# Attention on one core: VectorE's exponential in four instructions, ten groups instead of nine, and two banks for the last head

## The chip, the cores and the metric

The kernel runs on one core of a Trainium2 chip. A core has engines that run their own instruction streams in order and meet at semaphores: TensorE (PE; PEld is its weight load), VectorE (DVE), ScalarE (ACT), GpSimd (POOL) and SyncE (SP, which here only issues DMAs). SBUF is the working memory, PSUM holds what TensorE writes, in banks of 2 KB per partition. The metric is device time in microseconds (us); lower is better.

## The reference

Plain softmax attention over 8 x 8 heads, 512 queries and keys, 64 dimensions, all float32:

```python
scale = 1.0 / np.sqrt(q.shape[-1])
scores = np.einsum('bhqd,bhkd->bhqk', q, k) * scale
scores = scores - scores.max(axis=-1, keepdims=True)
attn = np.exp(scores)
attn = attn / attn.sum(axis=-1, keepdims=True)
return np.einsum('bhqk,bhkd->bhqd', attn, v)
```

The inputs are standard normal draws, and the kernel leaves out the subtraction of the maximum: it takes the exponential of the scaled score as it is, and divides at the end.

## The kernel before

**Tiles.** Heads go in 32 pairs `g` of two heads `h`. Per pair q, k and v are loaded by SP (256 KB each, up to seven pairs ahead), cast to float16 on GpSimd (`cast`, L435 and L445), and q and k are transposed on TensorE (L469); VectorE copies the transposed pair from PSUM to the tile `tqk` (L482). The scores of one head are taken with keys on the partitions, so one key block `c` of 128 keys gives a 128 x 512 block of scores, one bank. Two such blocks make a group `m`, a PSUM tile `st` of two banks (128 x 1024), and there are three such tiles. There are 128 groups; the last is done as two halves of 256 queries, so `m` runs to 128.

**The exponential** of a group is one ACTIVATE on ScalarE (L516) that writes the float16 tile `pt`. The groups listed in `ON_DVE` go to VectorE instead. For them TensorE first adds a constant to the scores by two matmuls of a constant tile `lift` (L497), and VectorE then runs `raise_` (L536), a multiply and a maximum that turns `st` into a float tile `z` whose upper bits are the exponent and whose lower 16 bits are a fraction f. That instruction releases the score tile. After it come the passes (L553), each a `scalar_tensor_tensor` over 128 x 1024 elements. Before the change there are four: y = (f + c0) f, y = (y + c1) f, y = (y + c2) f, and y c3 + z, whose result, stored as an unsigned integer in the tile `pd`, has in a 16-bit half of each word the float16 exponential.

**Values.** The float16 blocks are the weights of matmuls against v with a column of ones beside it (L588), so 65 columns come out: 64 dimensions and the sum. A unit is 128 queries of one head, four matmuls; seven units fill a bank, and VectorE's `normalise` then takes the reciprocal of the sums (L566) and multiplies (L568) into `ring`. For each finished head SP stores 128 KB. The last head is treated apart: `last_values` (L603) writes its four units as parts 0 to 3 into a score tile, parts 0 and 1 for key blocks 0 and 1 of all queries, part 2 for blocks 2 and 3 of the first 256 queries, part 3 for those of the last 256. `finish` (L617, L618) normalises each half, and its store goes out on SP's queue for the first half and on ScalarE's for the second.

**What sets the order.** The class `Plan` simulates the engines with fixed costs in nanoseconds, and the steps that it notes are emitted in that order for all engines. Its constants steer it:

- `PASS`, `PASSES` are the planned cost and number of passes of a group on VectorE.
- `KEEN` keeps the values of any head back until group number `m` has passed it.
- `CALM`: a cast planned after that time is given a wait on VectorE's latest instruction; one planned earlier starts when its data is there.
- `LATE_NORM`, `LATE_COPY`: VectorE begins a pass only if no norm or raise (copy) that is known to come would then be made later than this. In `step_dve`, `end` is the planned end of the pass, and all `ready` entries `x` must have `x[0] > end - late[x[1]]`.
- `BACKLOG`: TensorE waits up to `SOON` (80) for a score tile if ScalarE's planned work in hand is less than this.
- A pair with a group in `ON_DVE` has its v cast due 6000 later (`late` in `__init__`), and SP's later loads follow the casts.

In `last_values` before the change all four units share one bank of the score tile `o_last`.

Of the kernel before, what the change touches and what calls it, by code (L numbers as in the profile page):

```python
# [17 lines left out]
class Plan:  # L18
# [6 lines left out]
    COPY, NORM, RAISE = (601, 690), (307, 390), (1132, 1215)  # L25
    COPY_1 = (400, 190)
    NORM_COLUMN, PASS_DONE = 67, 80
    PASS, PASSES = 1133, 4
    OFFSET = 216
    FIRST_EXP = 4915  # L30
    STEP = 5
    CALM, KEEN = 9000, 4
    FIRST_UNIT = 4
    ON_DVE = (8, 24, 35, 41, 61, 68, 80, 94, 111)

    LATE_NORM, LATE_COPY, HURRY, SOON, BACKLOG = 1300, 1400, 900, 80, 1000
    SLACK, AHEAD = 0, 1

    CAST, CAST_DONE, TO_POOL = 557, 130, 150
# [3 lines left out]
    def __init__(self, groups, pairs, first):  # L43
# [26 lines left out]

        late = {grp[0][0] for m, grp in enumerate(groups) if m in self.ON_DVE}
        due = []
# [75 lines left out]
    def for_dve(self, m):  # L148
        return m in self.ON_DVE

# [192 lines left out]
def kernel(  # L343
# [7 lines left out]
    nc = tc.nc  # L351
    B, H, S, D = q.shape
    P = 128
    NI = S // P
    assert NI == 4 and D == 64 and S == 512
    scale = float(D) ** -0.5
# [45 lines left out]
    last = {}  # L402

    def source(src, g):
        b, h = g // ppb, 2 * (g % ppb)
        return src[b, h : h + 2].rearrange("h (p i) d -> p h i d", i=NI)
# [45 lines left out]
    def dve(ins):  # L452
        latest[:] = [ins]
        return ins
# [32 lines left out]
    def scores(m, on_dve):  # L487
# [35 lines left out]

    LIFT, STEP = (793.0 / 32, -0.039614853593207044 / 32), scale * 1.4426950408889634 * 1024
    QUARTIC = tuple(
        x * 65536.0**n
        for n, x in enumerate((-22.8615461, 17.9701791, 3.89093568)[::-1], 1)
    ) + (1.34267018e-02 * 1024 * 2.0**-64,)  # L530

    def raise_(m):
        r = raised[m]
# [12 lines left out]
    def pass_(m, s):  # L546
        r = raised[m]
        f = r["z"].bitcast(U16).rearrange("p x (s n) -> p x s n", n=2)[:, :, :, 0]
        if s == 0:
            r["y"] = wpool.tile([P, 2, S], FP32, tag="y", name=f"y_{m}")  # L550
        last = s == 3
        dve(
            nc.vector.scalar_tensor_tensor(  # L553
                out=r["bits"][:, :, :] if last else r["y"][:, :, :],
                in0=r["y"][:, :, :] if s else f,
                scalar=QUARTIC[s],
                in1=r["z"][:, :, :] if last else f,
                op0=AluOp.mult if last else AluOp.add,
                op1=AluOp.add if last else AluOp.mult,
            )  # L560
        )
# [34 lines left out]
    def last_values(part):  # L596
        if part == 0:
            o = ps_st.tile([P, 2, S], FP32, tag="st", name="o_last")
            last["o"] = o[:, 0, 0 : NI * (D + 1)].rearrange("p (x d) -> p x d", x=NI)
        o = last["o"]  # L600
        for c in (part,) if part < 2 else (2, 3):
            for x in (range(NI), range(NI), (0, 1), (2, 3))[part]:
                nc.tensor.matmul(  # L603
                    o[:, x, :],
                    blocks[(LAST, c, 1)][:, x * P : (x + 1) * P],
                    vps[LAST % NV][:, 1, c, :],
                    start=(c == 0 and x == 0),
                    stop=(c == NI - 1),
                    skip_group_check=True,
                )  # L610

    def finish(part):
        o = last["o"]
        n = slice(2 * part - 4, 2 * part - 2)
        ob = opool.tile([P, 2, D], FP32, tag="obl", name=f"obl_{part}")
        rc = opool.tile([P, 7, 1], FP32, tag="rc", name=f"rc_last_{part}")
        nc.vector.reciprocal(out=rc[:, 0:2], in_=o[:, n, D : D + 1])  # L617
        nc.vector.tensor_tensor(  # L618
            out=ob[:, :, :],
            in0=o[:, n, 0:D],  # L620
            in1=rc[:, 0:2].broadcast_to([P, 2, D]),
            op=AluOp.mult,
        )
        queue = (nc.sync, nc.scalar)[part - 2]
        queue.dma_start(out=source(out, LAST)[:, 1, n], in_=ob[:, :, :])
# [101 lines left out]
    with tc.manual_schedule():  # L727
        plan = Plan(groups, NP, 3)
        steps = plan.run()
        first_loads()  # L730
        for g, name in plan.first_loads:
            load(g, name)
        make_identity(nc, ident)
        nc.vector.memset(lift, LIFT[0])
        for p in (32, 96):
            nc.vector.memset(lift[p : p + 32], LIFT[1])
        for n in range(NV):
            nc.vector.memset(vps[n][:, :, :, D : D + 1], 1.0)
        first_pair()
        do = {  # L740
            "transposes": transposes,
            "scores": scores,
            "values": values,
            "load": load,
            "cast": cast_behind,
            "raise": raise_,
            "copy": lambda g, b: copy(g),
            "pass": pass_,
            "last": last_values,
            "finish": finish,  # L750
            "norm": lambda u, n, b: normalise(u, n),
        }
        for what, *args in steps:
            do[what](*args)
# [30 lines left out]
```

## Time and profile before

| what | value |
|---|---|
| time, three runs | 120.11, 120.23, 120.72 us; median 120.23 |
| profiled execution: its own time, as its span from first to last instruction | 118.6 us |
| TensorE busy | 105.0 us (89%) |
| VectorE busy | 103.7 us (87%) |
| ScalarE busy | 111.6 us (94%) |
| GpSimd busy | 57.5 us (48%) |
| HBM traffic | 25.17 MB read, 8.39 MB written, 283 GB/s |
| mean granted TensorE clock | 0.993 |

The profile is of one execution, and the page gives no other time for it than the span. Its groups name line, engine, operation, tile written <- tiles read, shape and count; behind the bar stand busy time, the mean duration of one instruction in ns, and the idle time of the engine just before them with what ended it. In the timeline the first two numbers are start and duration in us from the start of the span, xN says how many instructions are merged, and brackets give idle time before. Instructions of one engine overlap at their ends, so a duration is a little longer than the step from one to the next.

### The profile page before, as it was taken

Reading aid. Unit: us, or ns where it says so; the run is one execution under the profiler, and the core shown is the slowest. Engines: PE = TensorE matmul, PEld = TensorE weight load, DVE = VectorE, ACT = ScalarE, POOL = GpSimd, SP = SyncE. Lnnn points to the kernel's source line nnn. Section 1 sums busy time; section 2 is a strip of 40 time slices with the busy share of each in tenths; the row PEclk is TensorE's granted clock in tenths of the full one; section 3 lists DMA queues with packets and bytes.
Section 4 is the critical chain, followed back from the end, with each engine's and each line's share of the span. In section 5 each row is a group of like instructions: output and inputs, shape, how many; then the busy total and the mean of one; then the engine's idle time right before and its main releaser. Section 6 shows DMA issues by size and latency. Waiting matters only on the chain.

```text
span 118.6 us, 4088 instructions
## 1 busy us (share of the span) xinstructions
PE 105.0 (89%) x1577; PEld 66.4 (56%) x1577; DVE 103.7 (87%) x179; ACT 111.6 (94%) x124; POOL 57.5 (48%) x102
## 2 busy tenths in 40 slices
PE   7969987999799897989989998998899998998960
PEld 2626554755466454658545574675465674755750
DVE  3453999799999999998999999999999999998560
ACT  4699999999999999999999999999999999999960
POOL 2378731991547722555947255533645436524000
PEclk9999999999999999999999999999999999999997
DMA  3999999999999999999889957999899874231344
GB/s 101 305 352 380 378 380 383 383 379 378 367 302 326 350 365 355 327 371 358 250 297 275 299 169 255 342 364 293 266 309 373 275 253 164 91 122 63 109 163 134
DMA packets 35607, 33.83 MB, mean 285 GB/s; under 512 B 2691, under 2 KB 35587, under 8 KB 35587
## 3 DMA queue, kind: packets, MB, share of 16 engines
q1 hardware_dynamic: 35152, 33.24, 84.8%
q10 hardware_dynamic: 432, 0.33, 0.8%
q8 instruction: 12, 0.20, 0.8%
q14 instruction: 11, 0.07, 0.2%
HBM read 25.17 MB, written 8.39 MB: 283 GB/s over the span
## 4 chain that ended last, share of the span: by engine, by line
ACT 34%; PE 28%; DVE 16%; DMA 11%; issue 6%; SPq 1%; POOL 1%; ACTq 0%
ACT pt L516 32%; PE o L588 10%; PE st L511 10%; DMA k<-in_k_dram 8%; DVE y L553 5%; PE tp L469 4%; DVE tqk L482 3%; DVE ring L568 3%; DMA out_dram<-ring 3%; PE st_0a L636 3%; ACT pt L686 2%; DVE z L536 1%; DVE rc L566 1%; DVE pd L553 1%; SPq L429 1%
## 5 line engine op out<-in xcount | busy, mean ns | idle before, releaser
L516 ACT ACTIVATE pt<-st 128x1024 f16<-128x1024 f32 (+1 forms) x117 | 106.7, 1200 | 0.1
L511 PE MATMUL st<-tqk 64*128 64x512 f16 (+1 forms) x250 | 45.3, 379 | 7.1 <-ACT pt L516 5.4
L588 PE MATMUL o<-vp,pt 128*128 128x65 f16 x936 | 41.7, 194 | 0.0
L588 PEld LDWEIGHTS <-pt 128*128 128x128 f16 x936 | 35.4, 98 | 11.2 <-issue 8.5
L445 POOL CAST qkp<-k 128x512 f16<-128x512 f32 x31 | 19.1, 616 | 20.1 <-DVE y L553 5.5
L435 POOL CAST vp<-v 128x512 f16<-128x512 f32 x32 | 19.7, 619 | 16.6 <-DVE y L553 9.7
L511 PEld LDWEIGHTS <-tqk 64*128 64x128 f16 x250 | 13.7, 93 | 20.9 <-issue 13.8
L445 POOL CAST qkp<-q 128x512 f16<-128x512 f32 x30 | 18.5, 616 | 12.0 <-DVE y L553 7.0
L568 DVE TENSOR_TENSOR ring<-o,rc 128x448 f32<-128x448 f32 (+2 forms) x37 | 22.6, 612 | 1.3
L553 DVE SCALAR_TENSOR_TENSOR y<-y,z 128x1024 f32<-128x1024 f32 x18 | 22.1, 1228 | 0.0
L469 PE MATMUL tp<-ident,qkp 128*128 128x128 f16 x248 | 20.1, 220 | 0.9 <-DVE tqk L482 0.4
L482 DVE COPY tqk<-tp 128x1024 f16<-128x1024 f16 x30 | 20.5, 682 | 0.3 <-PE tp L469 0.3
L469 PEld LDWEIGHTS <-qkp 128*128 128x128 f16 x248 | 14.4, 97 | 8.9 <-issue 4.3
L553 DVE SCALAR_TENSOR_TENSOR y<-z 128x1024 f32<-128x1024 uint16 x9 | 12.1, 1340 | 0.0
L536 DVE TENSOR_SCALAR z<-st 128x1024 f32<-128x1024 f32 x9 | 11.0, 1219 | 1.1 <-PE st L511 0.9
L566 DVE RECIPROCAL rc<-o 128x7 f32<-128x7 f32 (+2 forms) x37 | 7.3, 196 | 4.9 <-PE o L588 4.9
L553 DVE SCALAR_TENSOR_TENSOR pd<-y,z 128x1024 uint32<-128x1024 f32 x9 | 11.2, 1242 | 0.0
L588 PE MATMUL o<-vp,pd 128*128 128x65 f16 x72 | 10.5, 195 | 0.1
L588 PEld LDWEIGHTS <-pd 128*128 128x128 f16 x72 | 7.0, 98 | 1.5 <-issue 0.9
L497 PE MATMUL st<-const-bfloat16-1.0,lift 64*128 64x512 bf16 x18 | 3.5, 383 | 0.5 <-ACT pt L516 0.5
L636 PE MATMUL st_0a<-const-bfloat16-1.0 128*128 128x512 bf16 (+1 forms) x11 | 3.3, 456 | 0.8 <-PEq L769 0.8
L636 PEld LDWEIGHTS <-const-bfloat16-1.0 128*128 128x128 bf16 x15 | 1.6, 122 | 2.4 <-issue 2.4
(48 smaller groups left out, 21.5 us busy)
## 6 DMA issues: line engine op xcount, KB each, us to landing
out_dram<-ring SPq DMA_DIRECT2D x63, 128.0 KB, 4.0
k<-in_k_dram SPq DMA_DIRECT2D x31, 256.0 KB, 5.1
q<-in_q_dram SPq DMA_DIRECT2D x31, 256.0 KB, 5.1
v<-in_v_dram SPq DMA_DIRECT2D x27, 256.0 KB, 5.2
v<-in_v_dram SPq DMA_DIRECT2D x10, 128.0 KB, 3.9
k<-in_k_dram ACTq DMA_DIRECT2D x2, 128.0 KB, 2.9
q<-in_q_dram SPq DMA_DIRECT2D x2, 128.0 KB, 2.7
out_dram<-obl SPq DMA_DIRECT2D x1, 64.0 KB, 1.6
```

The source lines that it names most:

```text
L435: return nc.gpsimd.tensor_copy(out=vps[g % NV][:, :, :, 0:D], in_=raw[g]["v"][:, :, :, :])
L445: return nc.gpsimd.tensor_copy(out=dst, in_=src[:, :, :, :])
L469: nc.tensor.transpose(tps[g][:, n, i, :], qkp[g][:, n, i, :], ident)
L482: nc.vector.tensor_copy(out=tqk[g][:, :, :], in_=tps.pop(g).rearrange("p n i c -> p n (i c)"))
L511: nc.tensor.matmul(st[:, x, cols], kc, qc[:, cols], start=not on_dve, stop=True)
L516: nc.scalar.activation(out=pt[:, :, cols], in_=st[:, :, cols], func=EXP, scale=scale)
L536: nc.vector.tensor_scalar(out=r["z"][:, :, :], in0=r["st"][:, :, :], scalar1=STEP, scalar2=2.0**17, op0=AluOp.mult, op1=AluOp.max,)
L553: nc.vector.scalar_tensor_tensor(out=r["bits"][:, :, :] if last else r["y"][:, :, :], in0=r["y"][:, :, :] if s else f, scalar=QUARTIC[s], ...
L566: nc.vector.reciprocal(out=rc[:, 0:n], in_=o[:, x : x + n, D : D + 1])
L568: nc.vector.tensor_tensor(out=ring[:, u % NU : u % NU + n, :], in0=o[:, x : x + n, 0:D], in1=rc[:, 0:n].broadcast_to([P, n, D]), op=AluOp. ...
L588: nc.tensor.matmul(os[u // 7][:, u % 7, :], blocks[(g, c, h)][:, y * P : (y + 1) * P], vps[g % NV][:, h, c, :], start=(c == 0), stop=(c == ...
L636: nc.tensor.matmul(dst[:, 0:n], ones[:, 0:P], ones[:, 0:n], start=True, stop=True)
```

## The change

The polynomial in f is written as a product of two quadratics, so that it takes three passes in place of four: y = (f + c0) f, then y = (y + c1) y, then y c2 + z. The constant in `lift` and the coefficients are new. `ON_DVE` has ten groups in place of nine, at other places, and five constants of the plan are set anew. In the last head the two halves of the queries go to the two banks of the score tile, and `finish` reads its own bank.

```diff
-    PASS, PASSES = 1133, 4
+    PASS, PASSES = 1133, 3
...
-    CALM, KEEN = 9000, 4
+    CALM, KEEN = 14000, 6
...
-    ON_DVE = (8, 24, 35, 41, 61, 68, 80, 94, 111)
-
-    LATE_NORM, LATE_COPY, HURRY, SOON, BACKLOG = 1300, 1400, 900, 80, 1000
+    ON_DVE = (8, 21, 29, 40, 54, 65, 77, 85, 90, 106)
+
+    LATE_NORM, LATE_COPY, HURRY, SOON, BACKLOG = 600, 1800, 900, 80, 1200
...
-    LIFT, STEP = (793.0 / 32, -0.039614853593207044 / 32), scale * 1.4426950408889634 * 1024
-    QUARTIC = tuple(
-        x * 65536.0**n
-        for n, x in enumerate((-22.8615461, 17.9701791, 3.89093568)[::-1], 1)
-    ) + (1.34267018e-02 * 1024 * 2.0**-64,)
+    LIFT, STEP = (793.0 / 32, -0.039907195352 / 32), scale * 1.4426950408889634 * 1024
+    QUARTIC = (7.77974906 * 2.0**16, -8.78105033 * 2.0**32, 4.4655924e-3 * 1024 * 2.0**-64)
...
-        last = s == 3
+        last = s == 2
         dve(
             nc.vector.scalar_tensor_tensor(
                 out=r["bits"][:, :, :] if last else r["y"][:, :, :],
                 in0=r["y"][:, :, :] if s else f,
                 scalar=QUARTIC[s],
-                in1=r["z"][:, :, :] if last else f,
+                in1=(f, r["y"][:, :, :], r["z"][:, :, :])[s],
                 op0=AluOp.mult if last else AluOp.add,
                 op1=AluOp.add if last else AluOp.mult,
...
-            last["o"] = o[:, 0, 0 : NI * (D + 1)].rearrange("p (x d) -> p x d", x=NI)
+            last["o"] = [
+                o[:, n, 0 : 2 * (D + 1)].rearrange("p (x d) -> p x d", x=2) for n in range(2)
+            ]
...
-                    o[:, x, :],
+                    o[x // 2][:, x % 2, :],
                     blocks[(LAST, c, 1)][:, x * P : (x + 1) * P],
                     vps[LAST % NV][:, 1, c, :],
-                    start=(c == 0 and x == 0),
+                    start=(c == 0 and x % 2 == 0),
...
-        o = last["o"]
+        o = last["o"][part - 2]
...
-        nc.vector.reciprocal(out=rc[:, 0:2], in_=o[:, n, D : D + 1])
+        nc.vector.reciprocal(out=rc[:, 0:2], in_=o[:, :, D : D + 1])
...
-            in0=o[:, n, 0:D],
+            in0=o[:, :, 0:D],
```

## The prediction

> **What bounds the kernel now.** I read the page's busy shares first, then ScalarE's and VectorE's groups with each form kept apart, then the waits, then stretches of the span, and last the timeline of the tail. Times are in microseconds.
>
> ```profile
> span 118.6 us, 4088 instructions
> PE 105.0 (89%) x1577; PEld 66.4 (56%) x1577; DVE 103.7 (87%) x179; ACT 111.6 (94%) x124; POOL 57.5 (48%) x102
> ```
>
> Three engines are near full, so a share alone decides nothing. The groups by form (busy, mean ns | idle before):
>
> ```profile
> L516 ACT ACTIVATE pt<-st 128x1024 f16<-128x1024 f32 x115 | 105.7, 1211 | 0.1
> ...
> L553 DVE SCALAR_TENSOR_TENSOR y<-y,z 128x1024 f32<-128x1024 f32 x18 | 22.1, 1228 | 0.0
> ...
> L553 DVE SCALAR_TENSOR_TENSOR y<-z 128x1024 f32<-128x1024 uint16 x9 | 12.1, 1340 | 0.0
> L553 DVE SCALAR_TENSOR_TENSOR pd<-y,z 128x1024 uint32<-128x1024 f32 x9 | 11.2, 1242 | 0.0
> L536 DVE TENSOR_SCALAR z<-st 128x1024 f32<-128x1024 f32 x9 | 11.0, 1219 | 1.1 <-PE st L511 0.9
> ```
>
> ScalarE has 0.1 of idle in front of 115 exponentials: it runs without a break. Its timeline gives the price of one slot:
>
> ```profile
> 5.92 1.98 ACT L686 ACTIVATE pt<-st 128x1024 f16<-128x1024 f32 x2
> 7.80 106.75 ACT L516 ACTIVATE pt<-st 128x1024 f16<-128x1024 f32 x117
> ...
> 36.42 21.18 ACT L516 ACTIVATE pt<-st 128x1024 f16<-128x1024 f32 x23
> ```
>
> An undisturbed stretch holds 23 whole groups in 21.18; the first of them lasts 1.02, so one more group costs (21.18 - 1.02) / 22 = 0.916. (The mean of 1211 ns is longer since neighbours overlap.) The whole run of 117, two of them halves of about 0.49, takes 106.75: (106.75 - 1.02 - 0.98) / 114 = 0.919. So all stalls of ScalarE together are about 114 x 0.0025 = 0.3. Whatever else the engines do, ScalarE's slots set the time of 4.95 to 114.55.
>
> The other two engines, in the stretch in which VectorE carries exponentials, and behind it (us, PE, PEld, DVE, ACT, POOL, clock, DMA, GB/s):
>
> ```profile
> 11.85:108.50 96.65, 88.62 (x1372) 56.83 (x1370) 94.03 (x137) 96.59 (x107) 50.21 (x85) 1.00 0.92 303
> 108.50:114.40 5.90, 5.75 (x110) 3.86 (x106) 3.25 (x9) 5.90 (x8) 0.62 (x1) 1.00 0.35 115
> ```
>
> VectorE is 97% full up to its last pass and half idle behind it; TensorE has 8 of 96.65 to spare, and the waits put 5.4 of its idle time to ScalarE not yet having released a score tile. The granted clock is full. The tail (start, duration):
>
> ```profile
> 112.55 2.00 ACT L516 ACTIVATE pt<-st 128x1024 f16<-128x1024 f32 x3
> ...
> 114.46 0.17 DVE L617 RECIPROCAL rc_last<-o_last 128x2 f32<-128x2 f32 x1
> ...
> 114.66 0.29 DVE L618 TENSOR_TENSOR obl<-o_last,rc_last 128x128 f32<-128x128 f32 x1
> 114.87 0.17 DVE L566 RECIPROCAL rc<-o 128x4 f32<-128x4 f32 x1
> 115.00 0.29 PE L603 MATMUL o_last<-vp,pt 128*128 128x65 f16 x4 [0.46 <-DVE obl L618]
> ...
> 115.08 0.42 DVE L568 TENSOR_TENSOR ring<-o,rc 128x256 f32<-128x256 f32 x1
> ...
> 115.42 0.16 DVE L617 RECIPROCAL rc_last<-o_last 128x2 f32<-128x2 f32 x1
> 115.61 0.29 DVE L618 TENSOR_TENSOR obl<-o_last,rc_last 128x128 f32<-128x128 f32 x1
> ...
> 115.94 0.35 ACTq L625 DMA_DIRECT2D out_dram<-obl  x1
> ```
>
> TensorE waits 0.46 for VectorE there, but VectorE itself runs from 114.46 to 115.90 with no gap over 0.03: the second finish stands behind the norm of four units, not behind TensorE.
>
> **The change, part by part.** All terms are differences within the profiled execution, whose own time is known as its span, 118.6. The three timed runs lie at 120.11 to 120.72, median 120.23; 1.6 of that median lies around the span, and I take it as unchanged.
>
> *One group from ScalarE to VectorE* (nine to ten): -0.916, on the path.
>
> *One pass fewer.* VectorE's exponentials cost 9 x (1.219 + 1.340 + 2 x 1.228 + 1.242) = 56.3 now. The new middle pass reads one float tile twice; no row shows that. The nearest rows are the float pass at 1.228 and the dearest single first pass, 1.637; the cheapest is 1.212. I take 1.228, the same width and types. Ten groups: 10 x (1.219 + 1.340 + 1.228 + 1.242) = 50.3, so VectorE sheds 6.0 (1.9 at the dear end). None is on the path while ScalarE is full; it pays for the next part.
>
> *Later thresholds.* LATE_NORM 1300 to 600 holds a pass back (1.133 in the plan) when a norm or raise is known to come within 0.53, so VectorE now idles at times. A norm is known at most 0.445 ahead. If each of 37 norms and 10 raises hit the worst, 37 x 0.445 + 10 x 0.53 = 21.8; at nothing hit, 0. VectorE becomes free about once in 1.2, so a norm is met in 0.445 / 1.2 = 37% of cases, with half of 0.445 lost: 37 x 0.37 x 0.22 = 3, and likewise 10 x 0.44 x 0.27 = 1.2. I take 4, which the shed 6.0 covers; without that cover, blocks on VectorE come later and the values that need them move back. LATE_COPY 1400 to 1800 lets a pass that must first wait for a cast begin all the same; a tqk copy behind it waits up to one pass, 1.23, but the transposes run a pair ahead, some 3.7 of ScalarE's slots. Nothing on the path.
>
> *Lift matmuls.* The tenth group adds two at L497: 18 take 3.5, so 0.39 of TensorE. Hidden in its 8 spare; uncovered, 0.39.
>
> *KEEN, CALM, BACKLOG.* The first values matmuls (9.19) already follow the scores of group 6, so KEEN of 6 moves nothing. CALM takes the wait behind VectorE from casts planned between 9 and 14 us; the first two-input pass is at 14.36, so they meet only the z pass, 1.225 with a cast beside it against a median of 1.218. Nothing; at most one cast, 0.62, in front of the first pass. SP's loads behind those casts move by as little. BACKLOG lets TensorE wait at most 0.08 for a score tile when ScalarE has up to 1.2 in hand. Nothing.
>
> *The new places.* ScalarE's stalls were 0.3 with nine groups; the worst, at 35.50, starts 1.42 after its neighbour where 0.904 is usual, but ends only 0.17 late, since starts had run ahead of ends (a group's record grows from 1.02 to at most 1.41 before such a gap). Ends for ten groups: -0.3 (all stalls gone) and +1.7 (ten like the worst). I take 0, nearest to the mean of 0.03 a group. The v casts of the pairs that now hold such a group are due 6 later in the plan, those of the pairs that no longer do 6 earlier; GpSimd's idle half (57.5 busy) takes the move, and SP's loads behind a moved cast have seven pairs of loads in hand. Without that cover a load slips by one cast, 0.62.
>
> *The tail.* With two banks the last four matmuls can start at 114.60 in place of 115.00. If VectorE's order stays, the second finish still stands behind the norm: 0. If the norm comes ahead of the first finish, the second can start at 114.95, and ends at 115.40 in place of 115.90: -0.5. What speaks for a move: now VectorE's last block is done only at 108.52, and its eight units of values (o<-vp,pd, 109.59 to 110.5, about 1.0 of TensorE) push the last scores and pair 30 back; the timeline has the scores of two groups together at 110.64, although the first group's tile was free a slot earlier. With 106 for 111 the last block comes five slots (4.6) and a pass earlier, and TensorE gains some 0.4 in front of the last units. I take half, -0.25: the first finish may still wait for the norm. SP's queue must issue the ring store and the first half's, 0.4 each, in that time; it can. The sum is -0.916 - 0.25 = -1.17: 119.1.
>
> Two pages of the Trainium skill bear on this. The Trainium skill's "ScalarE: Activation LUTs" (What ACT_TABLE_LOAD costs) gives 186 ns + 0.833 N for an ACTIVATE, with about 93 ns of overlap between neighbours: an estimate of 0.946 for 1024 elements; the trace has 0.916, and by the page the sum would be -1.20. The Trainium skill's "SBUF — State Buffer" (Who interferes with whom) speaks against part of the gain: an instruction of VectorE with two SBUF inputs, the new (y + c) y too, contends with a cast of GpSimd, and who issues first blocks the other. The trace agrees: 1.637 for a first pass that starts beside casts, 1.215 for one that is clear of them; CALM's unguarded casts fall under it, as the bounds above already have it.
>
> **The rivals.**
>
> *The slot alone.* VectorE's order at the end stays, or the wait for the bank was for the whole tile and the split does nothing: -0.92, 119.3. For it: no gap on VectorE from 114.46 on.
>
> *Stalls eat the slot.* A score tile in VectorE's hands leaves ScalarE two. A raise that comes due behind a running pass waits up to 1.22; ScalarE's run-ahead is 1.41 - 1.02 = 0.4, so such a group costs up to 0.8. One of them with the order of the tail kept: -0.92 + 0.8 = -0.1, 120.1. Against it: nine groups gave only 0.3.
>
> *Slower.* The same at three groups: 2.4 - 0.92 = +1.5, 121.7. It decides from 0.92 + 0.6 = 1.5 of stalls on, two such groups. For it: 85 and 90 are five slots (4.6) apart, 21 and 29 eight, while two groups need eight operations of 1.23 among copies and norms that fill nearly half of VectorE. Against it: 35 and 41 now overlap so and cost 0.17.
>
> **How the numbers follow.** A difference under 0.5% (0.6) is about what a measurement of this kernel cannot tell from none; so faster is below 119.63 and slower above 120.83. Chances: slot and tail 0.42 (119.1), slot alone 0.26 (119.3), stalls eat it 0.17 (119.7 to 120.8), slower 0.15. Faster 0.68, same 0.17, slower 0.15. The low end has all stalls gone and the whole tail: -0.92 - 0.3 - 0.5, 118.5. The high end, 120.5, is one group and a half at 0.8 over the 119.3 of the kept tail; beyond it lie the slower case and a little of the third, below the low end next to nothing: 0.2 in all.
>
> **What would show it.** Right: L516 with x114 whole groups and still about 0.1 idle; 10 each of z, y<-z, y<-y and pd, near 50.3 in all; an o_last group with no wait for obl; VectorE's stretch less than 97% full. The tail: the norm of 128x256 ahead of the first rc_last, and the last obl at most 1.1 behind the last ACTIVATE's end (now 1.35). Wrong: idle or late starts of ScalarE behind a raise, above all near groups 29 and 90; a VectorE still full, with its last pd later than 104; TensorE with values left after the last exponential.

## The result, and the profile after

The changed kernel takes 119.09 us (median of four runs, 118.64 to 119.28), the kernel before 120.36 beside it: 0.988 of the time, with a 95% interval of 0.985 to 0.991 (the two medians alone give 0.989). That is faster by 1.27, against a forecast of 119.1. Some executions were disturbed and slower; the times of the experiments are medians of the others, and of the profiles of nine_three, ten_four and drop_106_pad, which are of disturbed executions, only the closing sequence of the program is read.

The page of the changed kernel:

```profile
span 117.5 us, 4082 instructions
...
PE 105.0 (89%) x1579; PEld 66.5 (57%) x1579; DVE 98.2 (84%) x174; ACT 110.7 (94%) x123; POOL 58.4 (50%) x102
```

The groups by form that answer to those of before (busy, mean ns | idle before):

```profile
L516 ACT ACTIVATE pt<-st 128x1024 f16<-128x1024 f32 x114 | 104.7, 1297 | 0.0
...
L550 DVE SCALAR_TENSOR_TENSOR y<-y 128x1024 f32<-128x1024 f32 x10 | 12.4, 1240 | 0.0
L550 DVE SCALAR_TENSOR_TENSOR y<-z 128x1024 f32<-128x1024 uint16 x10 | 12.3, 1234 | 0.1
L533 DVE TENSOR_SCALAR z<-st 128x1024 f32<-128x1024 f32 x10 | 12.2, 1221 | 2.5 <-PE st L511 2.3
L550 DVE SCALAR_TENSOR_TENSOR pd<-y,z 128x1024 uint32<-128x1024 f32 x10 | 12.2, 1217 | 0.0
```

ScalarE has one group fewer and still no idle. VectorE's four kinds come to 49.1 for ten groups, where nine took 56.4. ScalarE's timeline:

```profile
5.17 0.60 ACT L685 ACTIVATE pt<-st_0a 128x512 f16<-128x512 f32 x1 [0.60 <-PE st_0a L678]
...
8.12 105.68 ACT L516 ACTIVATE pt<-st 128x1024 f16<-128x1024 f32 x116
```

The 116 take 105.68 where 117 took 106.75. One slot is (105.68 - 1.02 - 0.98) / 113 = 0.917, the price of before. The tail (here and below without the lines of the weight loads, PEld):

```profile
113.03 0.18 DVE L563 RECIPROCAL rc<-o 128x4 f32<-128x4 f32 x1 [0.29 <-PE o L585]
113.25 0.42 DVE L565 TENSOR_TENSOR ring<-o,rc 128x256 f32<-128x256 f32 x1
113.70 0.17 DVE L616 RECIPROCAL rc_last<-o_last 128x2 f32<-128x2 f32 x1
113.91 0.29 DVE L617 TENSOR_TENSOR obl<-o_last,rc_last 128x128 f32<-128x128 f32 x1
114.25 0.28 PE L602 MATMUL o_last<-vp,pt 128*128 128x65 f16 x4 [0.59 <-DVE obl L617]
...
114.57 0.17 DVE L616 RECIPROCAL rc_last<-o_last 128x2 f32<-128x2 f32 x1 [0.37 <-PE o_last L602]
114.78 0.29 DVE L617 TENSOR_TENSOR obl<-o_last,rc_last 128x128 f32<-128x128 f32 x1
115.10 0.35 ACTq L624 DMA_DIRECT2D out_dram<-obl  x1
```

The norm of four units now stands ahead of the first finish. But TensorE still waits for that finish, 0.59, although the last four matmuls write another bank, and VectorE now idles 0.37 for it.

Three stretches add up to the difference of the spans, 118.60 to 117.49:

| stretch | before | after | difference |
|---|---|---|---|
| start to first exponential | 4.95 | 5.17 | +0.22 |
| first exponential to end of last | 109.60 | 108.63 | -0.97 |
| end of last exponential to end of span (tail) | 4.05 | 3.69 | -0.36 |

The first differs between executions of all kernels here (4.71 to 5.24; calm_old, a run below with the same order of instructions, has 4.71). It is not a later landing of the first loads: their casts start at 3.25 here and at 3.36 before. The first two matmuls of scores start at 4.73 in place of 4.63 and take 0.40 in place of 0.28; why is open. The other two are the change. Below, "ScalarE's stretch" and "tail" mean the second and the third.

### The profile page after: what moved, and what is told of

Same layout as the page of the kernel before. It is cut to its first block, busy times and chain, and to the rows that moved or that the text cites. A ratio compares the mean times of both kernels' runs of the same rounds, so it can differ in the third digit from the quotient of the medians.

```text
span 117.5 us, 4082 instructions
## 1 busy us (share of the span) xinstructions
PE 105.0 (89%) x1579; PEld 66.5 (57%) x1579; DVE 98.2 (84%) x174; ACT 110.7 (94%) x123; POOL 58.4 (50%) x102
## 4 chain that ended last, share of the span: by engine, by line
ACT 44%; PE 24%; issue 12%; DVE 11%; POOL 3%; DMA 3%; SPq 1%; POOLq 0%; ACTq 0%
ACT pt L516 43%; PE st L511 8%; PE o L585 8%; DVE y L550 3%; PE st_0a L635 3%; DMA out_dram<-ring 3%; DVE z L533 2%; POOL qkp L445 2%; PE tp L469 2%; DVE ring L565 2%; DVE tqk L482 2%; DVE pd L550 1%; ACT pt L685 1%; PE st L678 1%; PE st L497 1%
## 5 line engine op out<-in xcount | busy, mean ns | idle before, releaser
L585 PE MATMUL o<-vp,pt 128*128 128x65 f16 x928 | 42.3, 194 | 0.4 <-DVE tqk L482 0.2
L585 PEld LDWEIGHTS <-pt 128*128 128x128 f16 x928 | 35.6, 98 | 12.1 <-issue 10.9
L435 POOL CAST vp<-v 128x512 f16<-128x512 f32 x32 | 20.3, 640 | 16.4 <-DVE y L550 7.6
L511 PEld LDWEIGHTS <-tqk 64*128 64x128 f16 x250 | 13.1, 93 | 18.2 <-issue 10.4
L469 PE MATMUL tp<-ident,qkp 128*128 128x128 f16 x248 | 19.6, 220 | 1.3 <-DVE tqk L482 0.6
L533 DVE TENSOR_SCALAR z<-st 128x1024 f32<-128x1024 f32 x10 | 12.2, 1221 | 2.5 <-PE st L511 2.3
L550 DVE SCALAR_TENSOR_TENSOR y<-y 128x1024 f32<-128x1024 f32 x10 | 12.4, 1240 | 0.0
L550 DVE SCALAR_TENSOR_TENSOR pd<-y,z 128x1024 uint32<-128x1024 f32 x10 | 12.2, 1217 | 0.0
L585 PE MATMUL o<-vp,pd 128*128 128x65 f16 x80 | 11.8, 195 | 0.0
L585 PEld LDWEIGHTS <-pd 128*128 128x128 f16 x80 | 7.8, 98 | 1.5 <-issue 0.8
```

What stands on the lines that cost most here:

```text
L435: return nc.gpsimd.tensor_copy(out=vps[g % NV][:, :, :, 0:D], in_=raw[g]["v"][:, :, :, :])
L469: nc.tensor.transpose(tps[g][:, n, i, :], qkp[g][:, n, i, :], ident)
L511: nc.tensor.matmul(st[:, x, cols], kc, qc[:, cols], start=not on_dve, stop=True)
L533: nc.vector.tensor_scalar(out=r["z"][:, :, :], in0=r["st"][:, :, :], scalar1=STEP, scalar2=2.0**17, op0=AluOp.mult, op1=AluOp.max,)
L550: nc.vector.scalar_tensor_tensor(out=r["bits"][:, :, :] if last else r["y"][:, :, :], in0=r["y"][:, :, :] if s else f, scalar=QUARTIC[s], ...
L585: nc.tensor.matmul(os[u // 7][:, u % 7, :], blocks[(g, c, h)][:, y * P : (y + 1) * P], vps[g % NV][:, h, c, :], start=(c == 0), stop=(c == ...
```

## The experiments

Each run's time stands beside the kernel before on the same chip; its median was 120.6 to 120.7 in all of these. A short diff goes against the changed kernel unless another is named.

### One bank again

```diff
-            last["o"] = [
-                o[:, n, 0 : 2 * (D + 1)].rearrange("p (x d) -> p x d", x=2) for n in range(2)
-            ]
+            last["o"] = o[:, 0, 0 : NI * (D + 1)].rearrange("p (x d) -> p x d", x=NI)
...
```

> The changed kernel with the last head's four units back in one bank, nothing else. Theory A (TensorE's wait of 0.59 for the first finish is for the whole score tile, so the split into banks does nothing): the last matmuls wait 0.6 as before, the time from the end of the last exponential to the end of the span stays 3.7, and the kernel is where the changed one is, 119.1. Theory B (the split is worth something that the wait hides, as the prediction's step on the tail has it): the tail grows by 0.25 to 0.5, 119.3 to 119.6.

119.16 (0.987, interval 0.983 to 0.991); tail 3.70. The tail, beside the one above:

```profile
113.92 0.28 PE L600 MATMUL o_last<-vp,pt 128*128 128x65 f16 x4 [0.59 <-DVE obl L615]
...
114.24 0.17 DVE L614 RECIPROCAL rc_last<-o_last 128x2 f32<-128x2 f32 x1 [0.38 <-PE o_last L600]
```

The same wait, the same idle, the same tail: the split into two banks of one tile did nothing. The wait goes by the tile, not by the bank: the next run takes it away with a second tile.

### A tile of its own

```diff
+        last["bank"] = bank
...
+            other = ps_x.tile([P, 7, D + 1], FP32, tag=f"x{1 - last['bank']}", name="o_other")
             last["o"] = [
-                o[:, n, 0 : 2 * (D + 1)].rearrange("p (x d) -> p x d", x=2) for n in range(2)
+                o[:, 0, 0 : 2 * (D + 1)].rearrange("p (x d) -> p x d", x=2),
+                other[:, 0:2],
             ]
```

> The changed kernel with the second half of the last head in a PSUM tile of its own (the bank that the units before have just left), so that the program has no wait of TensorE for the first finish. Theory A: that wait was the last one in the tail; the second finish starts right behind the first (0.37 of idle on VectorE gone), the last store goes out 0.37 earlier, tail 3.3 in place of 3.7, 118.7. Theory B (the last store is bound by its own landing or by the store of the first half, not by the wait): tail within 0.1 of 3.7, 119.1.

118.52 (0.982, interval 0.978 to 0.985); tail 3.31. It is the fastest kernel of the study, and was timed on the same chip as one_bank: its runs lie at 118.20 to 118.94, those of one_bank at 118.68 to 119.40. Of the 0.64 between the two medians the tails show 0.39.

```profile
113.33 0.17 DVE L619 RECIPROCAL rc_last<-o_last 128x2 f32<-128x2 f32 x1
113.48 0.30 PE L605 MATMUL o_other<-vp,pt 128*128 128x65 f16 x4 [0.19 <-ACT pt L516]
113.53 0.29 DVE L620 TENSOR_TENSOR obl<-o_last,rc_last 128x128 f32<-128x128 f32 x1
113.82 0.17 DVE L619 RECIPROCAL rc_last<-o_other 128x2 f32<-128x2 f32 x1
...
114.02 0.29 DVE L620 TENSOR_TENSOR obl<-o_other,rc_last 128x128 f32<-128x128 f32 x1
114.35 0.35 ACTq L627 DMA_DIRECT2D out_dram<-obl  x1
```

TensorE now waits for the last exponential alone, and writes one bank while VectorE reads another (113.53 on). The second finish follows the first without a gap. The Trainium skill's "PSUM — Partial Sum Buffer" (PSUM bank collisions raise a hardware error) has the rule that accesses of two engines must be kept apart by bank and quadrant. This trace agrees in so far as the two overlap here in different banks; what the same bank would do, no run here shows.

### The norm held back

The plan keeps the last norm waiting until the first finish is noted.

```diff
+        self.finished = False
...
-        now = [x for x in self.ready if x[0] <= t]
+        end = 8 * self.pairs - 4
+        held = lambda x: x[1] == "norm" and x[2][0] == end and not self.finished
+        now = [x for x in self.ready if x[0] <= t and not held(x)]
...
+                self.finished = True
```

> The changed kernel with the last norm of four units held back until the first finish is done, the order that the kernel before has. Nothing else moves. Theory A (the gain of 0.36 in the tail is the norm's move): tail 4.0 to 4.1 in place of 3.7, 119.5; both the last finish (0.1 to 0.6 later) and the landing of the last store, which then shares the queues with the ring store (1.8 in place of 1.55), are later. Theory B (the tail's gain is something else, for example TensorE's shorter backlog): tail at most 3.8, 119.1 to 119.2.

119.00 (0.986, interval 0.982 to 0.989); tail 3.79. Neither number of theory A held: the tail is 0.1 longer, not 0.3 to 0.4, and the time is not longer within what the runs can tell. Theory B it is.

```profile
113.33 0.29 DVE L621 TENSOR_TENSOR obl<-o_last,rc_last 128x128 f32<-128x128 f32 x1
113.54 0.17 DVE L567 RECIPROCAL rc<-o 128x4 f32<-128x4 f32 x1
...
113.68 0.28 PE L606 MATMUL o_last<-vp,pt 128*128 128x65 f16 x4 [0.58 <-DVE obl L621]
113.75 0.42 DVE L569 TENSOR_TENSOR ring<-o,rc 128x256 f32<-128x256 f32 x1
...
114.09 0.16 DVE L620 RECIPROCAL rc_last<-o_last 128x2 f32<-128x2 f32 x1
```

The norm now fills the idle that TensorE's wait leaves on VectorE. So as long as that wait is there, the norm's place is worth 0.1. The last finish ends 1.35 after the last exponential, as in the kernel before (1.27 in the changed one). What is left of the 0.36 is the landing of the last store: 1.82 after its issue before, 1.55 after the change, 1.57 here. In the kernel before, SP still issued ring stores at 114.38 and 114.76, behind the norm of seven units that ran at 113.72, and had another to issue at 115.77. That these slow the last store is argued from the order, not shown.

### Three passes, nothing else

The kernel before, with the new polynomial.

```diff
-    PASS, PASSES = 1133, 4
+    PASS, PASSES = 1133, 3
...
```

> The kernel before with three passes in place of four (new constants of the polynomial, PASSES 3) and nothing else: nine groups at the old places, the old constants of the plan. Theory A (ScalarE's slots set the time; VectorE's 6 to 11 us less of work are worth nothing by themselves): from first exponential to last 109.6 as before, within 0.2; the norm comes ahead of the first finish in the program's order, so the tail may give 0.3: 120.0 to 120.2. Theory B (VectorE, 97% full, was a bound of its own, and the shed passes are what makes the gain): 119.1 to 119.5 with nine groups.

120.62 (1.000, interval 0.997 to 1.003). Taking nine passes from an engine that is busy 97% of its stretch changes nothing by itself. VectorE was no bound; theory B is out. The 120.0 to 120.2 of theory A did not come either: the 0.3 in the tail is not to be seen in the time. In its profile the closing sequence (see below) takes 1.13 where it takes 0.84 in the kernel before, which would hide that 0.3 if the time follows it.

### Ten groups, four passes

```diff
-    PASS, PASSES = 1133, 3
+    PASS, PASSES = 1133, 4
...
-    wpool = ctx.enter_context(tc.tile_pool(name="work", bufs=2))
+    wpool = ctx.enter_context(tc.tile_pool(name="work", bufs=4))
...
```

> The changed kernel with the old polynomial of four passes for its ten groups (and four in place of two work tiles, since more groups are in flight). Theory A (the shed pass is not on the path by itself, but it alone makes room for the tenth group): ten groups at four passes cost VectorE 61 to 62.6 against 49 to 50, more than the 98.2 busy of the changed kernel leaves in its span; blocks come later and later, TensorE has values left behind the last exponential, and the kernel is 3 us or more over the changed one, 122 or more. Theory B (VectorE is not near its bound with ten groups): within 0.5 of 119.1.

126.7 (1.050, interval 1.047 to 1.052). Without the shed pass the tenth group costs far more than it brings. The two runs belong together: the pass is worth nothing, and is what the group is paid with.

### One group back

```diff
-    ON_DVE = (8, 21, 29, 40, 54, 65, 77, 85, 90, 106)
+    ON_DVE = (8, 21, 29, 40, 54, 65, 77, 85, 90)
```

> The changed kernel with nine of its ten groups on VectorE: the last, 106, goes back to ScalarE. Theory A (a group costs ScalarE one slot and nothing else): from first exponential to last 0.92 longer, 109.5 in place of 108.5, tail unchanged at 3.7, 120.0. Theory B (places and constants give part of the gain, or a group on VectorE also costs stalls): the difference is under 0.6 or over 1.2.

120.33 (0.997, interval 0.995 to 0.999): 1.24 over the 119.09 of the changed kernel, outside the range that I had given the slot alone. But the kernel before, too, was 0.36 slower beside this run than beside the changed kernel; by the two ratios the difference is 0.009, or 1.1, inside the range. The profile takes it apart. ScalarE's timeline:

```profile
5.00 0.60 ACT L685 ACTIVATE pt<-st_0a 128x512 f16<-128x512 f32 x1 [0.43 <-PE st_0a L678]
...
7.77 106.54 ACT L516 ACTIVATE pt<-st 128x1024 f16<-128x1024 f32 x117
```

Its stretch is 109.31. That of the changed kernel is 108.63, and 108.40, 108.40 and 108.45 in one_bank, two_tiles and norm_behind, whose order up to the tail is the same: 108.47 in the mean, so the group is worth 0.84. The tail is 4.13, 0.44 longer, but its last store lands just as long after the last exponential (2.86, against 2.85 in the changed kernel). The whole 0.43 lies behind the last landing: the span ends 1.27 after it, where it ends 0.84 after it in the kernel before and in the changed one.

### The closing sequence

Behind the last landing the program ends with a sequence of semaphore instructions and drains. In it GpSimd has one gap of 0.33 to 0.37 in some kernels and none in others. The trace has 203 to 209 GpSimd records in those without, 198 to 202 in those with it, and in each of the seven with it the gap stands between the 196th and the 197th record. This experiment adds four small memsets to GpSimd's stream near the start.

```diff
         make_identity(nc, ident)
+        pad = cpool.tile([P, 4], FP32, name="pad")
+        for n in range(4):
+            nc.gpsimd.memset(pad[:, n : n + 1], 0.0)
```

> The changed kernel with nine groups, as in drop_106, and four tiny memsets of a scratch tile more on GpSimd near the start. In the ten profiles so far the span ends 0.84 after the last landing in all kernels whose GpSimd stream has 203 or more records, and at least 1.13 in those with 198 to 202, with a gap of 0.33 to 0.36 between two of GpSimd's closing instructions that moves with that count. Theory A (GpSimd waits for its next block of instructions in its closing sequence, and the place of that is a matter of its instruction count): 0.84 again, 0.43 less than drop_106, about 119.9, which leaves 0.8 to 0.9 over the changed kernel, one slot of ScalarE. Theory B (the longer end belongs to the order of work at the end): 1.2 to 1.3 stays, 120.3.

The closing sequence has the numbers of theory A: 205 records, 0.84 from the last landing to the end, no gap. Its reason, a wait for the next block of instructions, can be looked for in the instruction fetches of the page. Those within the span, of the changed kernel first, of drop_106 second, and with the memsets third, are (packets, MB, share):

```profile
q14 instruction: 8, 0.07, 0.2%
```

```profile
q14 instruction: 7, 0.06, 0.1%
```

```profile
q14 instruction: 8, 0.07, 0.2%
```

One block of 8 KB more is fetched inside the span where the gap is gone. But in drop_106 that block comes too, only behind the gap: the gap lasts from 117.44 to 117.80, and the fetch starts at 118.50, just behind the end of the span. In all seven kernels with the gap it starts 0.70 to 0.98 after the gap has ended, and this queue fetches nothing in the gap. So GpSimd does not wait there for that block, and what it waits for stays open. The time did not follow: 120.28 (0.997, interval 0.994 to 0.999), against 120.33 without the memsets; the 119.9 that was expected is the low edge of the interval. So the gap and its dependence on the count are shown; that it is worth 0.4 of the time is not. The runs scatter from 119.58 to 120.86, and why they did not come down stays open.

### The old constants

```diff
-    CALM, KEEN = 14000, 6
+    CALM, KEEN = 9000, 4
...
-    LATE_NORM, LATE_COPY, HURRY, SOON, BACKLOG = 600, 1800, 900, 80, 1200
+    LATE_NORM, LATE_COPY, HURRY, SOON, BACKLOG = 1300, 1400, 900, 80, 1000
```

> The changed kernel with the five constants of the plan as before (LATE_NORM 1300, LATE_COPY 1400, BACKLOG 1000, CALM 9000, KEEN 4); polynomial, groups and places as changed. Theory A (the prediction's step: these constants are worth nothing on ScalarE's path; they move only the order near the end): ScalarE from first to last within 0.4 of 108.5, tail up to 0.4 longer, 119.1 to 119.8. Theory B (the places hold only with the constants): stalls of 1 or more on ScalarE, or values left behind the last exponential: 120.3 or more.

120.74 (1.002, interval 1.000 to 1.004): the whole gain is gone, with ten groups, three passes and the new places all there. Theory B's second half, values left behind the last exponential, it is. ScalarE's stretch is 108.87, but the tail is 5.16, of which 0.35 is the longer closing sequence. The values matmuls (line L585) by stretches, first the changed kernel, then this one (us, PE busy and count, PEld, clock, DMA, GB/s):

```profile
60.00:80.00 20.00, 7.57 (x168) 6.26 (x168) 1.00 0.93 294
80.00:100.00 20.00, 8.71 (x208) 7.31 (x208) 1.00 0.92 306
100.00:114.00 14.00, 7.00 (x172) 5.96 (x172) 1.00 0.35 114
```

```profile
60.00:80.00 20.00, 7.61 (x180) 6.51 (x180) 1.00 0.98 311
80.00:100.00 20.00, 6.97 (x172) 6.33 (x173) 1.00 0.63 210
100.00:114.00 14.00, 8.38 (x214) 7.22 (x210) 1.00 0.35 115
```

Between 80 and 100 TensorE does 36 values matmuls fewer, nine units, and has 42 more to do between 100 and 114; some are left behind the last exponential (ends at 113.71), and the norm that needs them is the last work on VectorE:

```profile
114.28 0.67 PE L585 MATMUL o<-vp,pt 128*128 128x65 f16 x16
...
115.41 0.42 DVE L565 TENSOR_TENSOR ring<-o,rc 128x256 f32<-128x256 f32 x1
```

What held TensorE up shows in its waits between 76 and 101 (total, times, longest); in the changed kernel there is no wait for a copy in that stretch:

```profile
PE tp L469 <- DVE tqk L482: 1.0, 2, 0.7
...
PE st L511 <- DVE tqk L482: 0.7, 1, 0.7
```

With the old threshold VectorE's passes run earlier, the last one ends at 101.37 against 105.57, and TensorE waits for the copies behind them. That is a matter of order more than of rest. VectorE up to that pass (us, busy and count, clock, DMA, GB/s), the changed kernel first, then this one:

```profile
11.85:101.37 89.52, 83.22 (x125) 1.00 0.97 317
```

```profile
11.85:101.37 89.52, 83.91 (x122) 1.00 0.94 313
```

It is idle for 6.30 there in the changed kernel and for 5.61 here (2.55 in the kernel before). But by 100 it has done 29 norms and 27 passes in the changed kernel, and 27 norms and 29 passes here.

With LATE_COPY, BACKLOG or KEEN alone set back the plan's steps are the same as in the changed kernel, and with LATE_NORM alone they are those of this run, but for the waits of casts that CALM sets. So only LATE_NORM orders anything; CALM has a run of its own. The plan's order holds for TensorE as well, and how much of the 1.65 is waiting for copies and how much TensorE's own order is not separated.

### CALM and KEEN alone

```diff
-    CALM, KEEN = 14000, 6
+    CALM, KEEN = 9000, 4
```

> The changed kernel with CALM and KEEN alone as before. The order of the program is the same instruction by instruction; the casts planned between 9 and 14 us have their waits on VectorE again. Theory A (these two are worth nothing, and what the old constants cost is LATE_NORM): 119.1, ScalarE from first to last 108.4 to 108.7, tail 3.7. Theory B (the late start of ScalarE at 9.04 that the run with the old constants showed, 0.45, comes from these waits): 0.4 to 0.5 more, 119.5, with a late exponential near 9 us.

119.10 (0.988, interval 0.985 to 0.990), the changed kernel's time; tail 3.69. ScalarE's stretch is 108.98, over the 108.4 to 108.7 of theory A: the late exponential near 9 us is there (0.57 lost). But in this execution the first one started at 4.71, 0.46 earlier than in the changed kernel, and the last ends at 113.69 against 113.80. The times (118.85 to 119.50) show nothing that hangs on the two constants; what the late exponential would cost behind a later start, no run here shows.

### The new constants in the kernel before

```diff
-    LATE_NORM, LATE_COPY, HURRY, SOON, BACKLOG = 1300, 1400, 900, 80, 1000
+    LATE_NORM, LATE_COPY, HURRY, SOON, BACKLOG = 600, 1800, 900, 80, 1200
```

with CALM and KEEN as changed; nine groups, four passes, old places.

> The kernel before with the five new constants alone: nine groups, four passes, old places. Theory A (the lower LATE_NORM trades rest of VectorE against earlier norms, and only the shed pass pays for that rest): blocks on VectorE come some 4 later, ScalarE and TensorE stall, values are left behind the last exponential: 121.5 to 123.5. Theory B (earlier norms are a gain in any case): 119.5 to 120.2.

122.89 (1.020, interval 1.016 to 1.024). With four passes LATE_NORM does give VectorE rest: between 11.85 and 101.37 it is idle for 5.48, against 2.55 in the kernel before. That has to be paid for, and there is nothing to pay with. (The profile is of the longest of the four executions, 123.96.) VectorE's last block ends at 112.69 in place of 108.52, and score tiles come back late:

```profile
57.52 25.95 ACT L516 ACTIVATE pt<-st 128x1024 f16<-128x1024 f32 x28 [0.39 <-PE st L511]
84.33 3.77 ACT L516 ACTIVATE pt<-st 128x1024 f16<-128x1024 f32 x4 [0.87 <-PE st L511]
88.53 28.59 ACT L516 ACTIVATE pt<-st 128x1024 f16<-128x1024 f32 x32 [0.43 <-PE st L511]
```

Here ScalarE does stand idle, as the rivals had it.

### Two groups too close

```diff
-    ON_DVE = (8, 21, 29, 40, 54, 65, 77, 85, 90, 106)
+    ON_DVE = (8, 21, 29, 40, 54, 65, 77, 85, 87, 106)
...
-    wpool = ctx.enter_context(tc.tile_pool(name="work", bufs=2))
+    wpool = ctx.enter_context(tc.tile_pool(name="work", bufs=4))
```

> The changed kernel with the group at 90 moved to 87, two slots behind the one at 85 (and four in place of two work tiles, since three groups are then in flight). It measures the rival's price. Rival (a raise that waits behind a pass takes a score tile away from ScalarE, 0.8 a group): a visible loss of ScalarE of 0.5 to 1.0 near there, 119.7 to 120.1. Theory A (the plan's order and ScalarE's run-ahead cover it, as they did at 35 and 41): 0.2 at most, 119.1 to 119.3.

120.02 (0.994, interval 0.992 to 0.997). ScalarE's timeline:

```profile
7.32 1.02 ACT L685 ACTIVATE pt<-st 128x1024 f16<-128x1024 f32 x1 [0.28 <-PE st L678]
8.24 69.77 ACT L516 ACTIVATE pt<-st 128x1024 f16<-128x1024 f32 x76
78.41 35.92 ACT L516 ACTIVATE pt<-st 128x1024 f16<-128x1024 f32 x40 [0.40 <-PE st L511]
```

At 78.41, with group 88, the first of ScalarE's behind the one moved to 87, it idles 0.40, and that group ends 1.42 after its neighbour in place of 0.917: 0.51 lost, within the rival's price and below its 0.8. Of the 0.93 over the 119.09 of the changed kernel (0.8 by the ratios), the closing sequence, 0.35 longer in this profile, is another part, if the time follows it. The loss at 7.32 is in the start, before any group of VectorE.

### An eleventh group

```diff
-    ON_DVE = (8, 21, 29, 40, 54, 65, 77, 85, 90, 106)
+    ON_DVE = (8, 21, 33, 40, 53, 65, 74, 83, 90, 99, 106)
...
-    wpool = ctx.enter_context(tc.tile_pool(name="work", bufs=2))
+    wpool = ctx.enter_context(tc.tile_pool(name="work", bufs=4))
```

> The changed kernel with eleven groups on VectorE, at places chosen so that ScalarE is not held up in the plan (8, 21, 33, 40, 53, 65, 74, 83, 90, 99, 106), and four in place of two work tiles. Theory A (behind ScalarE stands TensorE, whose values are now late because ten groups already leave VectorE little rest): ScalarE from first to last 107.6 to 108.0, but the tail grows by 0.9 or more since values are left behind the last exponential: 119.0 to 119.7. Theory B (ScalarE's slots stay the only bound): 118.2 with a tail of 3.7.

119.65 (0.993, interval 0.990 to 0.995). ScalarE gives its slot back once more, without a stall:

```profile
8.02 104.70 ACT L516 ACTIVATE pt<-st 128x1024 f16<-128x1024 f32 x115
```

Its stretch is 107.48, but the tail is 5.15. VectorE is busy 39.13 of the 40 between 60 and 100 (37.34 in the changed kernel), its last block ends at 110.34, and TensorE still has values of that block to do when the last exponential ends at 112.72:

```profile
112.65 0.26 PE L585 MATMUL o<-vp,pt 128*128 128x65 f16 x3
112.74 0.19 PE L585 MATMUL o<-vp,pd 128*128 128x65 f16 x1
...
113.29 0.67 PE L585 MATMUL o<-vp,pt 128*128 128x65 f16 x16
```

So with eleven groups ScalarE is not the bound at the end; the values are, and behind them VectorE's lateness. With ten it still is, once the wait for the first finish is gone: in two_tiles the last matmuls wait for the last exponential alone.

## Why the prediction was right, and where its working was wrong

That the median meets the forecast to 0.01 is in part luck. Of the forecast's terms ScalarE's stretch gave 0.05 more and the tail 0.11 more, most of that tail by a way that was not forecast; the start took 0.22 back, and the time fell by 1.27 where the span fell by 1.11.

**The slot** (-0.916): right. ScalarE's stretch fell by 0.97, the group's return (drop_106) lengthens it by 0.84, and the eleventh takes 0.92 to 1.15 off again (107.48 against 108.40 to 108.63).

**One pass fewer** (6.0 shed, nothing on the path): right in kind; it shed 7.3. The mis-sized term is the first pass: 1.340 was taken over from before, 1.234 was measured, and fewer of these passes now start beside a cast (5 of 10, where it was 7 of 9). The new middle pass, for which no row stood, took 1.240 against 1.228. That the pass is not on the path is shown by nine_three, that it pays for the group by ten_four.

**The later thresholds** ("Nothing on the path"): this step failed. The rest was sized at 4; beside the old constants the threshold adds 0.7 of idle (6.30 against 5.61), and only with four passes 2.9 (5.48 against 2.55). What was missed is what the order does: copies and norms that go ahead of passes come on time and keep TensorE at its values, and that decides the tail. The last raise comes 5.2 earlier than before (93.46 against 98.63), but the last pass ends only 2.9 earlier, where the prediction counted on five slots and a pass, 5.8, and 4.2 later than with the old constants. With the old constants the time is 120.74, 1.65 more. The kernel gained 1.27, and of its parts neither the group nor the threshold gives that without the other: it takes the slot, the threshold and the shed pass that makes room for them (ten_four, before_new_constants).

**The tail** (-0.25): the size was near, -0.36, and most of the mechanism was not. The norm did come ahead of the first finish, and TensorE's values were done earlier, as forecast. But the second finish does not follow the first; the rival's clause, that the wait was for the whole tile and the split does nothing, was the true one (one_bank). The last finish ends 1.27 after the last exponential, where at most 1.1 was to show the step right. The norm's place is worth 0.1 (norm_behind); the other 0.26 is an earlier landing of the last store, which no step had and whose cause is not shown. Had the split done what it is for, the tail would have been another 0.4 shorter (two_tiles), 118.5, the low end of the range.

**KEEN, CALM, BACKLOG and the lift matmuls** (nothing): right in the time, by calm_old, by the unchanged steps, and by TensorE's waits for score tiles, which fell from 5.4 to 3.5 and did not vanish.

**The new places** (0, between -0.3 and +1.7): right. ScalarE's stalls were about 0.25, of which 0.14 lay in the start. The rivals' mechanism exists (crowded, 0.51; before_new_constants), and these places avoid it. Ten groups at other places with the new constants were tried only in crowded, so what the places are worth beyond that is not shown. The test I gave, a last pd later than 104 as a sign of a VectorE still full, was a bad one: it ended at 105.57 with VectorE 93% busy up to there (97% before), since its passes stand behind norms and copies, not because it is full.

The Trainium skill's "ScalarE: Activation LUTs" (What ACT_TABLE_LOAD costs) put one slot at an estimated 0.946; the changed kernel has 0.917, so the rows were the better price here too.

## What to carry to other kernels

An engine that is busy 97% need not be the bound: ask which engine has no idle at all, price its slot, and then look at what the engines behind it leave undone when its last slot ends. Work shed from a hidden engine is worth nothing until something spends it, here on a tenth block and on an order that puts another engine's inputs ahead of the hidden engine's own passes. When two halves are split so that one engine need not wait for another, look in the new program or trace whether the wait is gone; here it went by the tile, and only a second tile removed it.

## What the runs showed of the hardware that was not expected

The closing sequence behind the last landing took 0.84 in the kernels with 203 or more GpSimd records and 1.13 or more in those with 202 or fewer, with a gap of 0.33 to 0.37 between GpSimd's 196th and 197th record each time, whichever instruction stood there. Four more small instructions near the start took the gap away (1.27 to 0.84). It is not a wait for the 8 KB instruction fetch that those spans lack, since that fetch starts 0.70 or more after the gap; what it is stays open. The time of that kernel did not fall, so its worth is open too.
